# The first modulation rows turned into columns one sum later, through the transposes' PSUM pool

## The chip, the cores and the metric

The kernel runs on one core of a Trainium2 chip. The metric is the device time of one execution in microseconds, the median of several runs. Five engines work side by side, each with a queue of its own that it works off in order: TensorE (PE, and PEld for its weight loads), VectorE (DVE), ScalarE (ACT), GpSimd (POOL) and SyncE (SP), which issues all DMAs here.

## The reference, cut to what matters

One layer of a hybrid backbone is computed for 128 context tokens and 2048 latent tokens of width 1024, all in float32. What the change touches is the modulation at its very start:

```
def modulation(cond, w_mod_l, b_mod_l):
    m = jax.nn.silu(cond) @ w_mod_l + b_mod_l
    return jnp.split(m[:, None, :], N_MOD, axis=-1)
...
    sh1, sc1, ga1, sh2, sc2, ga2 = mod
    h = rmsnorm(x, norm_mix_l) * (1.0 + sc1) + sh1
    o, s_new = mixer(h, s0, n_chunks, w_in_l, conv_l, a_log_l, dt_bias_l, o_norm_l, ws_l, bs_l, w_out_l)
    x = x + ga1 * o
    h = rmsnorm(x, norm_ffn_l) * (1.0 + sc2) + sh2
    x = x + ga2 * (jnp.square(jax.nn.relu(h @ w_ff1_l)) @ w_ff2_l)
```

There are two conditioning vectors, one for the context and one for the latent tokens. Of the six pieces of the modulation, the shift `sh1` and the scale `sc1` are wanted first: no input of the mixer exists before them.

## The kernel before, in words

The 2176 tokens are 17 tiles of 128 rows: tile 0 is the context, tiles 1 to 16 are the latent tokens. The first phase projects blocks of three tiles; the second runs the scans; the third and longest is the MLP, whose matmuls are the lines 220 to 222 with the output `f`.

At the start of the first phase stand four sums of modulation rows. `mod_columns` (L331) makes one of them: 512 columns of `silu(cond) @ w_mod`, over eight slices `k` of the 1024 inputs (L335), with the two conditions as two rows of the PSUM tile `pm`. ScalarE copies the two rows into the tile `mrow` (L337). Four transposes (L340) turn them into columns, 128 of the 512 values at a time, in another `pm` tile. VectorE adds the bias (L343) and, for the scale, adds 1 and multiplies by the norm's weight (L347). What comes out is `b1` (shift) and `a1` (scale), with one column for each slice `k`. The four calls, in the order of the program:

- row 1: shift, half 0 (slices 0 to 3), right behind its loads `m0`
- row 2: scale, half 0, from `m1`, behind the preparation of block 0
- rows 3 and 4: shift and scale, half 1 (slices 4 to 7), from `m2` and `m3`, behind columns 0 to 3 of block 0

The tile `mrow` has one buffer, `pm` two (`pm1`), and `pt` three. `pt` serves all other transposes of the phase, and in block 0 also the sums of the third projection unit. The two `pm` tiles later go to the first sum of `split_mod_steps` (L359, L360) and to the matmuls of `ab_block` (L609, L610).

`column(k)` (L469) prepares slice k of block 0: transposes of the three normalised tiles `x` into a `pt` tile (L482), scale and shift by ScalarE into `full` (L484), then a high and a low part by VectorE, `kH` (L487) and `kL` (L488). Each column is stored to DRAM (L500, L501). The projection units (`feature_tile`) multiply the columns with split weights in three matmuls (L220 to L222), k by k: three units run together over k = 0 to 3, then go on with 4 to 7. `first_half` (L405) scales the halo rows, which GpSimd copies into the edges of the columns (L477, L478). The weights come through `raw_w` (L184) and are split by `split_w` (L191 on ScalarE, L192 on VectorE). `norm_rows` squares (L318), takes the root (L177, L178) and scales (L320) a tile of x, loaded at L392; the tag `x` has three buffers, and the halo tile `xh` (L380, L387) holds one of them first.

The order on each engine isn't the program's. The whole program is handed to a planner (`schedule_with_timeline_sim=True`), which keeps a clock of its own, gives each engine the earliest instruction of the program that is ready by that clock, and hands out the buffers of a tag. Nothing in the first phase fixes an order by hand; in the second, `emit` adds dependences that do.

Of the kernel before, what the change touches and what calls it, by code (L numbers as in the profile page):

```python
# [14 lines left out]
ALU = mybir.AluOpType  # L15
# [3 lines left out]
P = 128  # L19
# [43 lines left out]
def hybrid_step(  # L63
# [7 lines left out]
    V, A, G, T = nc.vector, nc.scalar, nc.gpsimd, nc.tensor  # L71
# [42 lines left out]
    ident = cp.tile([P, P], F32, name="ident")  # L114
# [42 lines left out]
    vec = cp.tile([P, 73], F32, name="vec")  # L157
    a1 = cp.tile([P, 2, KT], F32, name="a1")
    b1 = cp.tile([P, 2, KT], F32, name="b1")
# [11 lines left out]
    def pm1():  # L171
        return pmp.tile([P, 512], F32, tag="pm", name="pm", bufs=2)
# [14 lines left out]
    def split_w(raw, pool=None, tag="w"):  # L187

        h = (pool or wp).tile([P, 512], F32R, tag=tag, name="wH")
        lo = (pool or wp).tile([P, 512], F32R, tag=tag, name="wL")  # L190
        A.copy(h, raw)  # L191
        V.tensor_tensor(out=lo, in0=raw, in1=f32(h), op=ALU.subtract)  # L192
        return h, lo
# [13 lines left out]
    def w512(name, dt=F32):  # L207
        return wp.tile([P, 512], dt, tag="w", name=name)
# [72 lines left out]
    with ExitStack() as ph:  # L281
# [8 lines left out]
        def pt():  # L290
            return ppt.tile([P, 512], F32, tag="pt", name="pt", bufs=3)
# [35 lines left out]
        def mod_load(half, c0):  # L327
            return [raw_w(w_mod[0, k * P : (k + 1) * P, c0 + half * 512 : c0 + half * 512 + 512])
                    for k in range(KT)]

        def mod_columns(raws, half, dst, bias, scaled):  # L331

            pm = pm1()
            for k in range(KT):
                T.matmul(pm[0:2, :], scond[:, k, :], raws[k], start=k == 0, stop=k == KT - 1)  # L335
            row = p1.tile([2, 512], F32, tag="mrow", name="mrow", bufs=1)
            A.copy(row, pm[0:2, :])  # L337
            pc = pm1()
            for i in range(4):
                T.transpose(pc[:, 2 * i : 2 * i + 2], row[:, i * P : (i + 1) * P], ident[0:2, 0:2])  # L340
            ks = slice(half * 4, half * 4 + 4)
            d = dst[:, :, ks]
            V.tensor_tensor(out=d, in0=pc[:, 0:8].rearrange("p (k c) -> p c k", c=2),  # L343
                            in1=bias[:, ks].unsqueeze(1).to_broadcast([P, 2, 4]), op=ALU.add)
            if scaled:
                for cd in range(2):
                    V.scalar_tensor_tensor(out=dst[:, cd, ks], in0=dst[:, cd, ks], scalar=1.0,  # L347
                                           in1=vec[:, 16 + half * 4 : 20 + half * 4], op0=ALU.add, op1=ALU.mult)

        def split_mod_steps(jc):  # L350

# [18 lines left out]
        m0 = mod_load(0, 0)  # L370
        load(out=vec, in_=v_columns)
        convw = vec[:, 32:68].rearrange("p (w a) -> p w a", w=3)
        m1 = mod_load(0, D)
        mod_columns(m0, 0, b1, vec[:, 0:8], False)


        xh = p1.tile([P, D], F32, tag="x", name="xh", bufs=3)[0:10, :]
# [19 lines left out]
        def load_w1(gi, ks):  # L397
            return [w1_raw(gi, k) for k in ks]
# [332 lines left out]
        m2 = mod_load(1, 0)  # L731
        m3 = mod_load(1, D)
        wr = load_w1(1, range(4))
        mod_columns(m1, 0, a1, vec[:, 8:16], True)
        W1[1] += [split_w(r) for r in wr]
        first_half(0)
        abr = p1.tile([P, KT, 16], F32, tag="abr", name="abr", bufs=1)
# [4 lines left out]
        for k in range(4):  # L742
            cols[k]()
            for u in us:
                u["main"][k]()
        mod_columns(m2, 1, b1, vec[:, 0:8], False)
        mod_columns(m3, 1, a1, vec[:, 8:16], True)
        W1[1] += [split_w(r) for r in wk]
        first_half(1)
        for k in range(4, KT):  # L750
# [176 lines left out]
    with ExitStack() as ph:  # L927
# [550 lines left out]
        for i, u in enumerate(units):  # L1478
# [3 lines left out]
            c = i % 2  # L1482
# [107 lines left out]
    def bank():  # L1590
        return psq.tile([P, 512], F32, tag="f", name="f", bufs=8)
# [19 lines left out]
    class Unit:  # L1611
# [121 lines left out]
        def turn(self):  # L1733

            ps = bank()
            for i in range(4):
                T.transpose(ps[:, i * P : (i + 1) * P], self.z0[:, i * P : (i + 1) * P], ident)
            z = w512("zt")
            A.activation(z, ps, AF.Square)
            store(out=z_d[0][0, :, :, 2 * self.jp : 2 * self.jp + 2, :],  # L1740
                  in_=z.rearrange("p (i m t) -> p i m t", i=2, m=2))
# [175 lines left out]
    m0 = {n: [e[0] for e in todo].index(n) for n in range(len(products))}  # L1917
# [43 lines left out]
    half = [p for p, e in enumerate(seq) if e[1] == NP][0]  # L1961
# [9 lines left out]
    for j, t in enumerate(range(8, -1, -1)):  # L1971
        st = h2_steps(t, bank, lambda: junk16, w512, own=own_tile if t == 0 else None)
        p = 16 + 19 * j // 2
# [123 lines left out]
```

## Time and profile before

| | |
|---|---|
| median of 3 runs | 2585.69 us (2585.39 to 2588.91) |
| the profiled execution | 2585.89 us, span 2584.2 us |
| TensorE busy | 2544.6 us, 98% |
| VectorE busy | 1785.2 us, 69% |
| ScalarE busy | 1193.2 us, 46% |
| GpSimd busy | 297.4 us, 12% |
| DMA | 579.77 MB, 224 GB/s on average |

The rows of a timeline give the start and the length in us, the engine, the line, the operation, the tile written and the tiles read, the shape and the count; in brackets stands the idle time ahead of it and what ended that. Consecutive instructions of one kind are merged into one row. Rows of SPq are DMA issues. A group of a view by tiles gives the least, the median and the greatest duration. The tile names are those of the program.

### The profile page before, as it was taken

The page shows a single profiled execution, that of the slowest core. Times are in us where ns is not written, and L with a number is a line of the kernel's source. Part 1 is how long each engine was busy: PE and PEld are TensorE (multiplying, and loading weights), DVE is VectorE, ACT ScalarE, POOL GpSimd, SP SyncE. Part 2 cuts the span into 40 slices and gives each one's busy share as a digit, 9 for nine tenths or more (in the row PEclk, how much of TensorE's full clock was granted, in tenths as well). Part 3 has the DMA queues.
Part 4 walks back from the last instruction along what each step waited for, and adds up shares of the span by engine and source line. Part 5 has one row for each costly group of instructions (what it writes and reads, how often), then busy time and mean ns, then how long its engine had stood idle before and what let it go on. Part 6 is the DMA issues. An engine that isn't in the chain of part 4 may idle for free.

```text
span 2584.2 us, 43725 instructions
## 1 busy us (share of the span) xinstructions
PE 2544.6 (98%) x15296; PEld 2134.3 (83%) x15296; DVE 1785.2 (69%) x3524; ACT 1193.2 (46%) x2758; POOL 297.4 (12%) x512
## 2 busy tenths in 40 slices
PE   8999999999999999999999999999999999999998
PEld 4999999788888878788888888888887888888887
DVE  5877746666667778895587886676665545675874
ACT  4755545554445557763355553333242433243441
POOL 3112112222222222321000000000000000000000
PEclk9999999999999999999999999999999999999999
DMA  8967637755555758996778788454379978786772
GB/s 297 293 217 214 201 115 226 230 166 171 162 173 177 223 180 250 289 310 208 266 221 251 219 288 278 139 152 146 115 224 373 331 267 297 248 257 213 231 254 103
DMA packets 533859, 579.77 MB, mean 224 GB/s; under 512 B 35500, under 2 KB 366684, under 8 KB 530054
## 3 DMA queue, kind: packets, MB, share of 16 engines
q1 hardware_dynamic: 533638, 576.98, 70.1%
q8 instruction: 120, 1.97, 0.3%
q14 instruction: 101, 0.83, 0.1%
HBM read 397.62 MB, written 179.22 MB: 223 GB/s over the span
## 4 chain that ended last, share of the span: by engine, by line
PE 52%; DMA 3%; DVE 1%; issue 1%; ACT 0%; POOL 0%; SPq 0%; DVEq 0%; POOLq 0%; ACTq 0%
PE f L220 16%; PE f L222 16%; PE f L221 16%; DMA r<-in_w_ff_dram 1%; PE pj L220 1%; PE pj L222 1%; DMA zraw<-z_d 1%; PE pj L221 1%; DMA traw<-in_w_ff_dram 0%; PE f L856 0%; PE pd L992 0%; PE pd L1096 0%; PE pd L1060 0%; PE pd L1097 0%; DVE o L1400 0%
## 5 line engine op out<-in xcount | busy, mean ns | idle before, releaser
L220 PE MATMUL f<-hop,zH 128*128 128x512 f32 x960 | 373.6, 390 | 1.9 <-ACT zH L1600 1.8
L222 PE MATMUL f<-hop,zL 128*128 128x512 f32 x960 | 373.6, 389 | 0.0
L221 PE MATMUL f<-hop,zH 128*128 128x512 f32 x960 | 373.2, 389 | 0.0
L220 PE MATMUL f<-hop,wH 128*128 128x512 f32 x896 | 351.6, 393 | 0.6 <-ACT wH L1747 0.6
L221 PE MATMUL f<-hop,wH 128*128 128x512 f32 x896 | 349.0, 390 | 0.0
L222 PE MATMUL f<-hop,wL 128*128 128x512 f32 x896 | 344.0, 390 | 0.0
L1600 ACT CAST zH<-zraw 128x512 fp32r<-128x512 f32 x240 | 147.2, 620 | 298.2 <-DMA zraw<-s_d 87.5
L220 PEld LDWEIGHTS f<-hop,zH 128*128 128x128 f32 x960 | 180.2, 188 | 40.4 <-ACT zH L1600 3.4
L222 PEld LDWEIGHTS f<-hop,zL 128*128 128x128 f32 x960 | 180.2, 188 | 39.1 <-DVE zL L1594 1.7
L221 PEld LDWEIGHTS f<-hop,zH 128*128 128x128 f32 x960 | 180.2, 188 | 37.1
L1594 DVE TENSOR_TENSOR zL<-zraw,zH 128x512 fp32r<-128x512 f32 x240 | 163.1, 689 | 68.6 <-ACT zH L1600 53.7
L222 PEld LDWEIGHTS f<-hop,wL 128*128 128x128 f32 x896 | 168.2, 188 | 35.6
L220 PEld LDWEIGHTS f<-hop,wH 128*128 128x128 f32 x896 | 168.5, 188 | 34.9 <-issue 1.2
L221 PEld LDWEIGHTS f<-hop,wH 128*128 128x128 f32 x896 | 168.5, 188 | 32.3
L222 PE MATMUL pj<-kH,wL 128*128 128x386 f32 (+2 forms) x568 | 190.5, 335 | 0.0
L220 PE MATMUL pj<-kH,wH 128*128 128x386 f32 (+2 forms) x568 | 189.2, 336 | 0.5 <-DVE kH L487 0.3
L221 PE MATMUL pj<-kL,wH 128*128 128x386 f32 (+2 forms) x568 | 189.4, 333 | 0.0
L178 POOL TENSOR_TENSOR r<-rsq,nhalf 128x1 f32<-128x1 f32 (+1 forms) x38 | 22.9, 602 | 1357.1 <-DVE rsq L177 1357.1
L1747 ACT CAST wH<-s 128x512 fp32r<-128x512 f32 x96 | 58.9, 620 | 170.1 <-DVE s L1594 157.0
L537 DVE SCALAR_TENSOR_TENSOR cv<-pj,vec,cv 128x384 f32<-128x384 f32 (+2 forms) x164 | 87.3, 540 | 57.8 <-ACT cv L534 56.5
L220 PEld LDWEIGHTS pj<-kH,wH 128*128 128x128 f32 x568 | 107.1, 189 | 5.1 <-issue 4.7
L221 PEld LDWEIGHTS pj<-kL,wH 128*128 128x128 f32 x568 | 107.4, 189 | 0.5
(408 smaller groups left out, 5718.6 us busy)
## 6 DMA issues: line engine op xcount, KB each, us to landing
zraw<-z_d SPq DMA_DIRECT2D x212, 256.0 KB, 4.5
raw<-in_w_ff_dram SPq DMA_DIRECT2D x128, 256.0 KB, 4.7
hop<-hop_d SPq DMA_DIRECT2D x28, 1024.0 KB, 15.4
z_d<-c SPq DMA_DIRECT2D x96, 256.0 KB, 2.5
zraw<-s_d SPq DMA_DIRECT2D x96, 256.0 KB, 5.3
raw<-in_w_mod_dram SPq DMA_DIRECT2D x80, 256.0 KB, 4.0
r<-in_w_ff_dram SPq DMA_DIRECT2D x80, 256.0 KB, 5.7
s_d<-s SPq DMA_DIRECT2D x64, 256.0 KB, 3.1
```

The lines of the kernel that those rows point to most:

```text
L178: G.tensor_tensor(out=out, in0=t[:np_, :n], in1=nhalf[:np_, :n], op=ALU.pow)
L220: T.matmul(ps, lh, rh, start=first and i == 0, stop=False, skip_group_check=more)
L221: T.matmul(ps, lh, rl, start=False, stop=False, skip_group_check=more)
L222: T.matmul(ps, ll, rh, start=False, stop=last and i == n - 1, skip_group_check=more)
L537: V.scalar_tensor_tensor(out=cv[:, o : o + m], in0=ps[:, s + sh : s + sh + m], scalar=convw[:, w, j : j + 1], in1=cv[:, o : o + m], op0=AL ...
L1594: V.tensor_tensor(out=out, in0=a, in1=b, op=op)
L1600: A.copy(h, src)
L1747: A.copy(h, s2)
```

## The change

`mod_columns` no longer turns its row. It makes the sum and the copy, and hands back a function `turn` that does the rest: the transposes, now in a tile of `pt`, the addition and the multiplies. Each turn is called behind the next row's sum and copy. Row 3's sum moves up, ahead of columns 0 to 3; row 4's stays behind them, and the turns of rows 3 and 4 stand behind it.

```
             row = p1.tile([2, 512], F32, tag="mrow", name="mrow", bufs=1)
             A.copy(row, pm[0:2, :])
-            pc = pm1()
-            for i in range(4):
-                T.transpose(pc[:, 2 * i : 2 * i + 2], row[:, i * P : (i + 1) * P], ident[0:2, 0:2])
...
+            def turn():
+                pc = pt()
+                for i in range(4):
+                    T.transpose(pc[:, 2 * i : 2 * i + 2], row[:, i * P : (i + 1) * P], ident[0:2, 0:2])
+                ks = slice(half * 4, half * 4 + 4)
+                d = dst[:, :, ks]
+                V.tensor_tensor(out=d, in0=pc[:, 0:8].rearrange("p (k c) -> p c k", c=2),
+                                in1=bias[:, ks].unsqueeze(1).to_broadcast([P, 2, 4]), op=ALU.add)
+                if scaled:
+                    for cd in range(2):
+                        V.scalar_tensor_tensor(out=dst[:, cd, ks], in0=dst[:, cd, ks], scalar=1.0,
+                                               in1=vec[:, 16 + half * 4 : 20 + half * 4], op0=ALU.add, op1=ALU.mult)
+
+            return turn
...
-        mod_columns(m0, 0, b1, vec[:, 0:8], False)
+        turn = mod_columns(m0, 0, b1, vec[:, 0:8], False)
...
         wr = load_w1(1, range(4))
-        mod_columns(m1, 0, a1, vec[:, 8:16], True)
+        turn2 = mod_columns(m1, 0, a1, vec[:, 8:16], True)
+        turn()
+        turn = mod_columns(m2, 1, b1, vec[:, 0:8], False)
+        turn2()
         W1[1] += [split_w(r) for r in wr]
         first_half(0)
...
-        mod_columns(m2, 1, b1, vec[:, 0:8], False)
-        mod_columns(m3, 1, a1, vec[:, 8:16], True)
+        turn2 = mod_columns(m3, 1, a1, vec[:, 8:16], True)
+        turn()
+        turn2()
         W1[1] += [split_w(r) for r in wk]
         first_half(1)
```

More of the change, by code (lines that the diff above doesn't have):

```diff
@@ L337, in mod_columns @@
             A.copy(row, pm[0:2, :])
-            pc = pm1()
-            for i in range(4):
[L340 to L348, printed above, removed]
+            def turn():
[11 more added lines that the diff above has]
+            return turn
         def split_mod_steps(jc):
```

## The prediction

> **What bounds the kernel now.** I read the page's line of busy time first, then the busy time by stages (columns: stretch, its length, busy time and instructions of PE, PEld, DVE, ACT, POOL, granted clock, DMA share, GB/s).
>
> ```profile
> PE 2544.6 (98%) x15296; PEld 2134.3 (83%) x15296; DVE 1785.2 (69%) x3524; ACT 1193.2 (46%) x2758; POOL 297.4 (12%) x512
> ```
>
> ```profile
> 41.00:100.00 59.00, 57.55 (x346) 55.56 (x347) 50.90 (x135) 42.94 (x124) 12.38 (x24) 1.00 0.82 260
> 200.00:300.00 100.00, 100.00 (x603) 94.84 (x602) 72.08 (x138) 55.98 (x177) 17.50 (x41) 1.00 0.68 211
> 1240.00:1700.00 460.00, 460.00 (x2139) 383.21 (x2138) 346.08 (x573) 204.49 (x417) 5.21 (x9) 1.00 0.75 239
> ```
>
> TensorE is idle for 2584.2 − 2544.6 = 39.6 us of the span. From 41 us on the first phase keeps it busy for 57.55 of 59 us and then 100 of 100, the last phase 460 of 460. So what TensorE saves before 41 us is handed down nearly whole, and what another engine saves counts only where TensorE waits for it. TensorE's timeline up to there holds all that the change can reach directly.
>
> ```profile
> 4.19 9.37 PE L335 MATMUL pm<-raw,scond 128*2 128x512 f32 x16 [4.19 <-DMA raw<-in_w_mod_dram]
> 14.31 0.38 PE L340 MATMUL pm<-ident,mrow 2*128 2x2 f32 x4 [0.76 <-ACT mrow L337]
> 14.62 7.03 PE L335 MATMUL pm<-raw,scond 128*2 128x512 f32 x16
> 21.57 0.66 PE L387 MATMUL pt<-ident,xh 10*128 10x10 f32 x8
> 22.16 0.33 PE L482 MATMUL pt<-ident,x 128*128 128x128 f32 x1
> 23.35 0.33 PE L482 MATMUL pt<-ident,x 128*128 128x128 f32 x1 [0.85 <-DVE x L320]
> 23.61 0.41 PE L340 MATMUL pm<-ident,mrow 2*128 2x2 f32 x4
> 23.94 7.03 PE L335 MATMUL pm<-raw,scond 128*2 128x512 f32 x16
> 31.69 0.41 PE L340 MATMUL pm<-ident,mrow 2*128 2x2 f32 x4 [0.72 <-ACT mrow L337]
> 32.02 7.03 PE L335 MATMUL pm<-raw,scond 128*2 128x512 f32 x16
> 38.98 0.33 PE L482 MATMUL pt<-ident,x 128*128 128x128 f32 x1
> 39.77 0.40 PE L340 MATMUL pm<-ident,mrow 2*128 2x2 f32 x4 [0.46 <-ACT mrow L337]
> ...
> 41.16 0.59 PE L220 MATMUL pj<-kH,wH 128*128 128x388 f32 x2 [0.33 <-DVE kH L487]
> 41.59 0.34 PE L220 MATMUL pt<-kH,wH 128*128 128x388 f32 x1
> 41.77 0.82 PE L482 MATMUL pt<-ident,x 128*128 128x128 f32 x6
> ```
>
> All four sums (L335) already run ahead of the first projection matmul at 41.16: the planner has pulled the third and the fourth up, although the program has them behind columns 0 to 3. Around them TensorE waits three times for the row's copy by ScalarE (0.76, 0.72, 0.46), once for a normalised tile (0.85), once for the first column (0.33): 3.1 us together, the ceiling of a direct gain.
>
> **The change part by part.** Nothing is added or removed: 64 sum matmuls, 16 transposes, 4 copies, 4 additions, 4 fused multiplies and every DMA stay. The transposes and what follows them move one sum back, the third sum moves up in the program (on the engine it is there already), and the columns take their banks from the three of `pt` instead of the two of `pm`.
>
> First turn. The second sum starts 14.62 − 13.56 = 1.06 us after the first ends (4.19 + 9.37 = 13.56): the copy, then transposes that take 14.62 − 14.31 = 0.31 of the engine. With the transposes behind it, it can start at 13.56 if its rows are there.
>
> ```profile
> 5.71 5.58 SPq L184 DMA_DIRECT2D raw<-in_w_mod_dram  x8
> 16.44 9.99 SPq L184 DMA_DIRECT2D raw<-in_w_mod_dram  x16
> ...
> DMA to landing us min/median/max: 4.7/5.4/5.8
> ```
>
> The last of its eight loads is issued by 11.3 and landed by 11.3 + 5.8 = 17.1, before the sum reaches it, so the sum ends at 13.56 + 7.03 = 20.6 and the turn at 20.9.
>
> Third sum. The halo transposes keep their place (22.16 − 21.57 = 0.59), so it could begin at 21.5. Its first load lands at 16.44 + 5.4 = 21.8 by the median; the others follow 9.99 / 16 = 0.62 apart, and the sum uses one in 7.03 / 8 = 0.88. I take 21.8 to 28.8, against the old end of 23.94 + 7.03 = 30.97. The 0.85 for the normalised tile falls inside it.
>
> Fourth sum. The second row's turn (0.31) and the two early transposes of x (some 0.5) go ahead, then it runs from 29.6 to 36.6, against 39.05 before; its last load lands by 26.43 + 5.8 = 32.2, in time.
>
> What is late next is the third tile of x, whose load stands late in SP's queue, and the way from it to the first projection:
>
> ```profile
> 28.21 0.33 SPq L392 DMA_DIRECT2D x<-in_x_sample_dram  x1
> 34.13 1.06 ACT L318 ACTIVATE junk<-x 128x1024 bf16<-128x1024 f32 x1 [0.64 <-DMA x<-in_x_sample_dram]
> 36.45 0.75 DVE L320 TENSOR_SCALAR x<-x,r 128x1024 f32<-128x1024 f32 x1
> 39.63 0.90 ACT L484 ACTIVATE full<-pt,b,a 128x128 f32<-128x128 f32 x2
> 40.11 0.23 DVE L487 CAST kH<-full 128x128 fp32r<-128x128 f32 x1 [1.51 <-ACT full L484]
> ```
>
> The tile is ready at 36.45 + 0.75 = 37.2, whatever the sums do. Before, its transpose came at 38.98 because the fourth sum held the engine until then; afterwards it can come at 37.2, and the first projection at 37.2 + (41.16 − 38.98) = 39.4: 1.8 earlier. The third and fourth rows' turns (2 × 0.31) then still have to run behind that point, where they ran ahead of it: net 1.8 − 0.6 = **1.2 us**. From below: 0, if the planner keeps the transposes where they wait for the same copies. From above: 3.1, if all the five waits go.
>
> Costs that I set to nothing, and their cover. The columns of half 0 come at about 29 instead of 24.5; behind them stand the halo's scaling on VectorE and its copies on GpSimd, which are wanted by the first column at 39, so 10 us cover them. SP's queue holds nothing that needs these columns before column 0's stores. The row has one buffer, so each copy now waits for the turn of the row before; ScalarE has nothing else to do but the squares and the first weight splits. If that cover went, the second split would be late by one copy, 0.57.
>
> The other half is less safe. Behind 41.59, where the third unit's first matmul takes its bank of `pt`, the transposes of columns 1 and 2 follow at 41.77, though two of the three tiles had been normalised since 23.35: a bank of `pt` is claimed in program order. In the new program the turns of rows 3 and 4 claim theirs behind column 3, and the fourth row's copy waits for the third's turn. So the columns of half 1, added at 40.25 before, come when columns 2 and 3 have left their banks. The rows that price this:
>
> ```profile
> 40.25 0.16 DVE L343 TENSOR_TENSOR a<-pm,vec 128x8 f32<-128x8 f32 x1
> ...
> 42.30 1.72 ACT L484 ACTIVATE full<-pt,b,a 128x128 f32<-128x128 f32 x4 [1.27 <-PE pt L482]
> 43.84 0.49 PE L482 MATMUL pt<-ident,x 128*128 128x128 f32 x3
> 45.73 0.93 ACT L484 ACTIVATE full<-pt,b,a 128x128 f32<-128x128 f32 x2
> 50.98 0.51 PE L220 MATMUL pj<-kH,wH 128*128 128x388 f32 x2
> ```
>
> Columns 1 and 2 are activated from 42.30 to 44.0, so until 42.2 when all is 1.8 earlier; column 3, whose transposes stand at 43.84, takes the bank of column 1, and the third row's turn that of column 2. From there the bare chain is turn 0.31, copy 0.57, turn 0.31, addition 0.16, multiplies 0.24, column 4's activation 0.93 and its two casts 0.7: 3.2 us, ready at 45.4. The matmuls of k = 4 start at 50.98 − 1.8 = 49.2. The slack is 3.8 us, and I take no stall. From below it is 0. From above each of the six steps stands behind one column's whole work on its engine: 2.45 on TensorE and VectorE ((50.98 − 41.16) / 4, the pace of the columns), 1.5 on ScalarE (0.93 and a weight split of 0.6); two steps on each make 12.8 of waits, a stall of 12.8 − 3.8 = 9.0.
>
> **Sum.** The profiled execution took 2585.89; 2585.89 − 1.2 = 2584.7. The median of the runs shown is 0.2 below it, so a median of 2584.5 is forecast.
>
> A rule that speaks against the change, as the trace has it first: in the scan TensorE once stood idle for 5 us, and then ran at half the granted clock for 3.4.
>
> ```profile
> 920.07 0.69 DVE L1437 TENSOR_TENSOR tmp<-pm,row 128x512 f32<-128x512 f32 x1 [5.33 <-DMA row<-mod_d]
> 920.82 1.11 PE L1413 MATMUL pm<-ident,ob 128*128 128x128 f32 x4 [5.04 <-DVE tmp L1437]
> ```
>
> ```profile
> 916.80:920.30 3.50, 0.00 (x0) 0.00 (x0) 0.23 (x1) 0.00 (x0) 0.03 (x1) 1.00 0.60 203
> 920.30:923.70 3.40, 2.88 (x23) 2.63 (x24) 3.40 (x6) 1.73 (x5) 0.00 (x0) 0.50 0.61 234
> ```
>
> The new order would leave TensorE with little to do from 36.6 to 37.2 and from 37.6 to 39.4. [...]
>
> **The rivals.**
>
> No gain (2585.9). The transposes keep waiting: x's third tile is later than I put it, or the turn lands where it was. For it: SP's order is the planner's, and the tile sets the end of the stage. Against it: the copy's waits have no other cause.
>
> [...]
>
> Half 1 is late (2589.8; slower than before). Place: the matmuls of k = 4. Price: the waits in the six steps less the slack of 3.8. It is slower than before from 3.8 + 1.2 = 5.0 us of waits on, slower by 0.2% from 10.2 on; midway between 5.0 and 12.8 the stall is 5.1, so 2584.7 + 5.1. For it: VectorE is busy with 50.90 of 59 us there. Against it: it needs most steps to meet full queues.
>
> The scan's order changes. The planner lays out the whole program again, and a start that is 1 to 2 us earlier can swap two loads. The stall at 920.82 hangs on one late row for L1437 (5.04 idle, and half of the 2.88 busy us at half clock, 1.4: 6.5). Without it 2584.7 − 6.5 = 2578.2; with a second one like it, 2591.2. For it: it is an accident of the queue. Against it: that stage's order hangs on dependences written by hand.
>
> **How the numbers follow.** Chances: forecast 0.47 (2584.5, its own range 2582.6 to 2585.6), no gain 0.18, clock 0.05, half 1 late 0.13, stall gone 0.13, second stall 0.04. A measurement of this kernel can tell about 0.2%, 5.2 us, from no change: faster is below 2580.5, slower above 2590.9. Faster has the stall gone, 0.13. Slower has the second stall, 0.04, and 0.06 of half 1 late. Same: 0.77. The range from 2579 to 2591 leaves out most of the stall gone (0.10), and what lies past 2591 of the other two (0.08).
>
> **What would show it.** Right: the second sum starts at about 13.6 with no wait for a copy; the fourth ends near 36.6; the first projection matmul stands near 39.4; PE's busy time is unchanged at 2544.6 and the span shorter by about 1. Right for half 1: the turns of rows 3 and 4 stand between the columns' transposes behind 41, and PE shows no wait at k = 4. Wrong: a wait of TensorE over 1 us between 37 and 60 us, a clock below 1.00 before 100 us, the third x tile's load at another place in SP's queue, or a shift of the stretches between 470 and 1240 us that the start does not explain.

## The result, and the profile after

The changed kernel is slower. Its median is 2594.53 us (2593.15 to 2599.43, 7 runs), beside 2588.63 us (2585.39 to 2591.81, 7 runs) of the kernel before on the same chip: a ratio of 1.0028, with a 95% interval of 1.0018 to 1.0037, or some 7 us with 5 to 10 as bounds. The forecast was 0.05% faster. The profiled execution took 2594.53 us, its span is 2592.8 us, against 2584.2 us before; these 8.6 us are more than the 7 of the ratio, since the profiled execution of the kernel before was one of its faster ones.

In the new source the lines stand 1 to 7 further down: the transposes of a turn are L341, the addition L344, the halo copies L480 and L481, the transposes of x L485, the scan's L1437 is L1444. `make_masks` (L135, L137), which the prediction did not speak of, makes the masks of the scan on GpSimd; `abW` (L760) holds what the split sum (L362) and `ab_block` multiply with.

The first fence is the page's line of busy time; the second the busy time by stages of the changed kernel, in the columns of the same view before.

```profile
PE 2547.5 (98%) x15296; PEld 2135.6 (82%) x15296; DVE 1787.3 (69%) x3524; ACT 1194.4 (46%) x2758; POOL 293.8 (11%) x512
```

```profile
38.50:41.90 3.40, 3.40 (x13) 3.12 (x13) 1.28 (x6) 1.21 (x4) 0.00 (x0) 0.50 1.04 345
41.00:100.00 59.00, 56.07 (x328) 52.85 (x327) 48.44 (x133) 41.63 (x116) 13.22 (x24) 0.99 0.70 226
100.00:140.00 40.00, 35.92 (x224) 34.22 (x224) 30.27 (x61) 21.98 (x65) 6.00 (x33) 1.00 0.92 304
200.00:300.00 100.00, 100.00 (x602) 94.58 (x601) 71.63 (x137) 53.51 (x169) 17.66 (x42) 1.00 0.61 193
925.90:932.80 6.90, 4.23 (x27) 3.78 (x28) 4.95 (x8) 3.07 (x8) 0.00 (x0) 0.51 0.57 200
1240.00:1700.00 460.00, 459.68 (x2135) 382.47 (x2134) 346.02 (x571) 204.38 (x416) 5.20 (x9) 1.00 0.74 236
```

The same 40 us from 100 on in the kernel before:

```profile
100.00:140.00 40.00, 39.50 (x242) 38.06 (x241) 31.34 (x64) 23.89 (x77) 10.87 (x36) 1.00 0.80 259
```

TensorE has the same work. It does 56.07 us of it between 41 and 100 us, where 57.55 were done before, and 35.92 between 100 and 140 us, where it was 39.50. From 200 on it is as full as ever. Between 38.5 and 41.9 the granted clock is 0.50. So the first phase loses in three places, all before 140 us.

TensorE's timeline shows first that the start went as the change meant it, and then where it waits:

```profile
4.34 15.59 PE L335 MATMUL pm<-raw,scond 128*2 128x512 f32 x32 [4.34 <-DMA raw<-in_w_mod_dram]
...
20.38 0.38 PE L341 MATMUL pt<-ident,mrow 2*128 2x2 f32 x4
21.02 3.60 PE L335 MATMUL pm<-raw,scond 128*2 128x512 f32 x8 [0.26 <-DMA raw<-in_w_mod_dram]
...
25.25 10.46 PE L335 MATMUL pm<-raw,scond 128*2 128x512 f32 x24
...
37.77 0.48 PE L362 MATMUL pm<-wH,abW 128*128 128x512 f32 x1 [1.79 <-DVE abW L760]
38.71 0.98 PE L220 MATMUL pj<-kH,wH 128*128 128x388 f32 x2
...
43.49 0.41 PE L341 MATMUL pt<-ident,mrow 2*128 2x2 f32 x4
...
46.65 0.41 PE L341 MATMUL pt<-ident,mrow 2*128 2x2 f32 x4
...
54.49 0.62 PE L220 MATMUL pj<-kH,wH 128*128 128x388 f32 x2 [1.43 <-POOL kH L480]
...
56.35 0.45 PE L221 MATMUL pj<-kL,wH 128*128 128x388 f32 x1 [0.35 <-POOL kL L481]
```

The first two sums run without a break (32 matmuls from 4.34 to 19.93), the other two nearly so (until 35.71), and the first projection matmul stands at 38.71 instead of 41.16: 2.4 us gained. Then the turns of rows 3 and 4 come at 43.49 and 46.65, where both had run by 40.2 before, and at 53 to 56 us TensorE waits 1.43 and 0.35 us for copies by GpSimd. The view of waits, each group with its total, count and longest time, adds what follows until 140 us:

```profile
PE pj L220 <- DVE cv L540: 3.5, 2, 2.4
PE pj L220 <- POOL kH L480: 1.4, 1, 1.4
PE pj L612 <- DVE cv L540: 0.9, 1, 0.9
...
PE pj L221 <- POOL kL L481: 0.3, 1, 0.3
```

The 3.5 and 0.9 us are waits for a bank of `pj` that VectorE's convolution (L540) has not emptied yet.

How the lag grows is read from the starts of the same matmul in both traces. The changed kernel's 70th projection matmul, at 59 us before, is 2.0 us late; the 208th, at 88, 1.4; the 346th, at 128, 6.2; the 691st, at 209, and the 1728th and last, at 432, 6.1. The first matmul of the MLP, at 1245, is 8.3 late, the last 8.6. So 6.1 us come from the first 130 us, and 2.2 from the scan. Its stall is still there:

```profile
928.57 1.12 PE L1420 MATMUL pm<-ident,ob 128*128 128x128 f32 x4 [5.36 <-DVE tmp L1444]
```

It is 5.36 us long against 5.04, and the half clock behind it lasts for the whole of 925.90:932.80 (0.51 above), twice as long as the 3.4 us of before. e4 and e17 below have some 6.8 us at half clock there too (an estimate from the mean clock: 0.96 in 905:920 and 0.72 in 920:930 in e4, 0.98 and 0.69 in e17) and are not slower, so it is not put down to the change.

GpSimd's timeline, of the changed kernel and then of the kernel before, shows why the copies were late:

```profile
48.08 0.72 POOL L135 TENSOR_SCALAR_AFFINE_SELECT sg<-one 128x128 f16<-128x128 f16 x1 [13.68 <-DVE a L348]
48.75 4.59 POOL L135 TENSOR_SCALAR_AFFINE_SELECT bd<-one 128x128 f16<-128x128 f16 x5
...
54.14 0.65 POOL L480 CAST kH<-halH 128x1 fp32r<-128x1 f32 x4
54.75 0.90 POOL L137 TENSOR_SCALAR_AFFINE_SELECT bd<-bd 128x128 f16<-128x128 f16 x2
55.60 1.37 POOL L481 CAST kL<-halL 128x1 fp32r<-128x1 f32 x4
```

```profile
42.42 1.16 POOL L477 CAST kH<-halH 128x1 fp32r<-128x1 f32 x4 [6.33 <-DVE halH L410]
43.52 0.94 POOL L478 CAST kL<-halL 128x1 fp32r<-128x1 f32 x4
48.23 0.97 POOL L135 TENSOR_SCALAR_AFFINE_SELECT sg<-one 128x128 f16<-128x128 f16 x1 [3.77 <-DVE one L129]
49.16 2.61 POOL L135 TENSOR_SCALAR_AFFINE_SELECT bd<-one 128x128 f16<-128x128 f16 x5
```

Before, GpSimd copied the edges of columns 4 to 7 at 42.4 and made the masks of the scan (L135, L137) from 48.2 on. Now the scale of half 1 is ready only at 48.1, and the masks stand ahead in GpSimd's queue. They also take longer, 4.59 us for five against 2.61. The edges are there at 57.0 instead of 44.5.

```profile
47.09 0.17 DVE L344 TENSOR_TENSOR a<-pt,vec 128x8 f32<-128x8 f32 x1
...
47.92 0.17 DVE L348 SCALAR_TENSOR_TENSOR a<-a,vec 128x4 f32<-128x4 f32 x2
48.13 1.24 DVE L410 TENSOR_SCALAR hal<-hal,a,b 128x10 f32<-128x10 f32 x4
...
49.62 0.41 DVE L413 CAST halH<-hal 128x40 fp32r<-128x40 f32 x1
...
50.41 0.34 DVE L414 TENSOR_TENSOR halL<-hal,halH 128x40 fp32r<-128x40 f32 x1
```

VectorE scaled the halo rows at once (L410) and had split them by 50.8 (L413, L414). Without the masks ahead of them, GpSimd could have begun the copies then.

### The profile page after: what moved, and what is told of

The parts are those of the page before. It is cut to its first block, busy times and chain, and to the rows that moved or that the text cites. A ratio compares the mean times of both kernels' runs of the same rounds, so it can differ in the third digit from the quotient of the medians.

```text
span 2592.8 us, 43725 instructions
## 1 busy us (share of the span) xinstructions
PE 2547.5 (98%) x15296; PEld 2135.6 (82%) x15296; DVE 1787.3 (69%) x3524; ACT 1194.4 (46%) x2758; POOL 293.8 (11%) x512
## 4 chain that ended last, share of the span: by engine, by line
PE 54%; DMA 1%; DVE 1%; issue 1%; ACT 0%; POOL 0%; SPq 0%; DVEq 0%; POOLq 0%; ACTq 0%
PE f L220 16%; PE f L222 16%; PE f L221 16%; PE pj L220 1%; PE pj L222 1%; PE pj L221 1%; DMA zraw<-z_d 1%; PE f L863 0%; PE pd L999 0%; DMA traw<-in_w_ff_dram 0%; PE pd L1103 0%; DMA r<-in_w_ff_dram 0%; PE pd L1067 0%; PE pd L1104 0%; DVE o L1407 0%
## 5 line engine op out<-in xcount | busy, mean ns | idle before, releaser
L221 PEld LDWEIGHTS f<-hop,zH 128*128 128x128 f32 x960 | 180.2, 188 | 37.2
L222 PEld LDWEIGHTS f<-hop,wL 128*128 128x128 f32 x896 | 168.2, 188 | 35.7
L1754 ACT CAST wH<-s 128x512 fp32r<-128x512 f32 x96 | 58.9, 620 | 169.7 <-DVE s L1601 156.5
L540 DVE SCALAR_TENSOR_TENSOR cv<-pj,vec,cv 128x384 f32<-128x384 f32 (+2 forms) x164 | 87.0, 540 | 58.7 <-ACT cv L537 57.5
```

The costliest lines, as they stand in the source:

```text
L221: T.matmul(ps, lh, rl, start=False, stop=False, skip_group_check=more)
L222: T.matmul(ps, ll, rh, start=False, stop=last and i == n - 1, skip_group_check=more)
L540: V.scalar_tensor_tensor(out=cv[:, o : o + m], in0=ps[:, s + sh : s + sh + m], scalar=convw[:, w, j : j + 1], in1=cv[:, o : o + m], op0=AL ...
L1754: A.copy(h, s2)
```

## The experiments

All ratios are to the kernel before, timed between the runs of the changed kernels on the same chip. The theory was that half 1 is the cause: its turns claim banks of `pt` behind columns 2 and 3, so its scale is late, and its edges with it. The rivals: the half clock at 38.5 us, the masks on GpSimd, and the order of TensorE's work that the planner takes.

**Which part of the change.** e3 takes the pool alone and leaves the turns where they were, e4 takes the delayed turns alone and leaves the pool:

```
 e3, in the kernel before      e4, in the changed kernel
-            pc = pm1()        -                pc = pt()
+            pc = pt()         +                pc = pm1()
```

> The kernel before with the columns in the pool of the transposes, each row turned at once as before. Theory A: the turns of rows 3 and 4 then claim their banks behind column 3, half 1 is as late as in the changed kernel, and the waits for the copies (0.76, 0.72, 0.46) stay: 4 to 8 us slower than before. Rival (the pool is innocent, the one sum's delay or the moved third sum costs the time): within 2 us of before.

> The changed kernel with the columns in the old pool pm: one sum later, but no claim of a bank of pt. Theory A: half 1 is turned ahead of the columns, its waits are gone, and the second sum still starts with no wait for the copy: 0 to 2 us faster than before, 5 to 8 faster than the changed kernel. Rival (the delay of one sum itself costs): as slow as the changed kernel.

e3 took 2593.43 us, a ratio of 1.0024 (1.0014 to 1.0034); e4 2587.19 us, 0.9999 (0.9990 to 1.0008). To within 0.1% the delay costs nothing, and the pool alone costs about as much as the whole change. Next, the pool for one half at a time:

```
 e6   +                pc = pt() if half == 0 else pm1()
 e7   +                pc = pt() if half == 1 else pm1()
```

> The changed kernel with rows 1 and 2 turned in pt, rows 3 and 4 in pm. Theory A2 (the claims of pt by rows 3 and 4, behind column 3, are what costs): half 1 is turned ahead of the columns, the first units end near 61 us as before, and the time is that of the kernel before within 2 us, unless the clock falls ahead of the first projection, which adds 1.7 for each 3.4 us at half. Rival (any four claims of pt upset the order): as slow as the changed kernel, +6.

> The mirror: rows 1 and 2 turned in pm, rows 3 and 4 in pt. Theory A2: half 1 is late as in the changed kernel, the halo copies stand behind the masks, the first units end near 68 us: +4 to +7 against before. Rival (rows 1 and 2 cost the time): near before.

e6: 2587.91 us, 1.0001 (0.9992 to 1.0011). e7: 2592.49 us, 1.0017 (1.0007 to 1.0027). To within 0.1%, only half 1 matters. The first copies of its edges on GpSimd, in e6 and in e7:

```profile
40.73 0.54 POOL L480 CAST kH<-halH 128x1 fp32r<-128x1 f32 x4 [6.07 <-DVE halH L413]
```

```profile
52.57 0.65 POOL L480 CAST kH<-halH 128x1 fp32r<-128x1 f32 x4
```

**What is costly about half 1.** e2 takes the masks out of the way, by making them at the very start:

```
         wr = load_w1(1, range(4))
+        make_masks()
         turn2 = mod_columns(m1, 0, a1, vec[:, 8:16], True)
...
-        make_masks()
```

> Only the place of the masks changes: built before the loads of m2 and m3, so GpSimd is free when the halo rows of half 1 are ready. Theory A in its narrow form (the masks in front of the halo copies are the wait): the waits for kH and kL at 53 to 56 us (1.78) go, the rest stays, about 2 us less than the changed kernel. In its wide form (the later waits at 66 and 130 us follow from it too): 4 to 5 us less. Rivals B and C: less than 1 us.

It took 2593.26 us, 1.0022 (1.0012 to 1.0032): nothing was gained. Its timelines of GpSimd and VectorE, and VectorE's busy time over the longest of the copies:

```profile
50.55 7.13 POOL L480 CAST kH<-halH 128x1 fp32r<-128x1 f32 x4 [15.86 <-DVE halH L413]
57.62 0.54 POOL L481 CAST kL<-halL 128x1 fp32r<-128x1 f32 x4
```

```profile
56.78 0.61 DVE L491 TENSOR_TENSOR kL<-full,kH 128x128 fp32r<-128x128 f32 x2
67.98 0.61 DVE L615 COPY absb<-pm 32x128 f32<-32x128 f32 x2 [10.59 <-PE pm L613]
```

```profile
51.65:57.40 5.75, 2.59 (x17) 2.30 (x15) 5.74 (x18) 3.97 (x9) 5.75 (x3) 1.00 0.60 195
```

GpSimd began the copies at 50.55, as soon as the halo rows were split, but four copies of one element per partition took 7.13 us, where e6 needed 0.54. The second of them alone lasted 5.79 us and ended at 57.44. VectorE worked almost without a break until then (5.74 of 5.75 us) and stopped at 57.39. So the masks were only one of two things that stood in the way. The other is read from the two ends alone: the second copy ended 0.05 us behind VectorE's whole run, and not between two of its instructions. This is no rule in these traces: in the kernel before, GpSimd's eight copies between 42.42 and 44.46 took 0.20 to 0.66 us each beside a VectorE that was busy for all of these 2.04 us, and each ended 0.04 us after one of VectorE's instructions. Why the one in e2 lasted through the whole run stays open.

e16 puts the question the other way: the masks stay, and ScalarE makes the edges of columns 4 to 7.

```
                 for col, j in hc:
-                    G.tensor_copy(kH[:, col : col + 1], f32(halH)[:, k, j : j + 1])
-                    G.tensor_copy(kL[:, col : col + 1], f32(halL)[:, k, j : j + 1])
+                    edge = A.copy if bi == 0 and k >= 4 else G.tensor_copy
+                    edge(kH[:, col : col + 1], f32(halH)[:, k, j : j + 1])
+                    edge(kL[:, col : col + 1], f32(halL)[:, k, j : j + 1])
```

> The changed kernel, with the halo copies of columns 4 to 7 on ScalarE in place of GpSimd. Theory 'GpSimd': the late columns cost through these copies, which stand behind the masks and are held up by VectorE's unbroken run; on ScalarE they take their turn at about 51, the waits of 1.43 and 0.35 near 53 and 56 us go, and the time falls to that of the kernel before or at most 1.5 us over it (2586 to 2589). Theory 'late columns': the columns are late whoever copies their edges; then TensorE still waits over 1 us between 48 and 60 us and the time stays 3 us or more over the kernel before.

2590.49 us, 1.0009 (1.0000 to 1.0019). ScalarE's timeline, and TensorE's waits until 140 us:

```profile
48.91 0.47 ACT L481 CAST kH<-halH 128x1 fp32r<-128x1 f32 x4 [0.49 <-DVE halH L413]
...
50.80 0.27 ACT L482 CAST kL<-halL 128x1 fp32r<-128x1 f32 x2
```

```profile
PE pj L220 <- DVE cv L541: 3.0, 3, 1.1
PE pt L553 <- ACT ev L596: 2.2, 1, 2.2
```

The time lies between the two theories. The edges are there at 51.1 instead of 57.0, although the turn of row 4 is still late (the scale is ready at 46.9), and the waits for GpSimd are gone. What is left is 2.4 us over the kernel before. The trace has it in later waits: `pj` banks that VectorE empties late, and 2.2 us for ScalarE near 126 us, which itself waits 3.80 us there for the store of an earlier `ev`. The clock of this trace did not fall at 38 us (1.00 in 38.50:41.90, against 0.50 in the changed kernel's), which is a part of what it gains on that trace: 1.7 us by an estimate, half of the 3.40 busy us at half clock.

**The order of the units.** Ahead of the third unit's last matmul TensorE does 48 projection matmuls into `pj` in the kernel before, which are the first two units' own (24 each), and 68 in the changed kernel, 20 of them of later units. (The expectations speak of 67 or 68 of the fourth unit; 48 of these are the first two's.) e1 turns half 1 early, but still in `pt`:

```
         turn2()
+        turn2 = mod_columns(m3, 1, a1, vec[:, 8:16], True)
+        turn()
+        turn2()
         W1[1] += [split_w(r) for r in wr]
...
-        turn2 = mod_columns(m3, 1, a1, vec[:, 8:16], True)
-        turn()
-        turn2()
         W1[1] += [split_w(r) for r in wk]
```

> Theory A (half 1 comes late): the turns of rows 3 and 4 stand behind column 3 in the claims of pt, so the halo copies of slices 4 to 7 fall behind the masks on GpSimd (waits of 1.43 and 0.35 at 53 to 56 us) and VectorE's work is pushed together later (1.15 at 66, 2.36 at 130). With the fourth sum and both turns ahead of the columns all of these waits are gone: 4.5 to 6 us less than the changed kernel, span about 2587. Rival B (the half clock from 38.5 to 41.9, after the wait ahead of the first projection, is the main loss): that wait stays, so at most 2 us less, span about 2591. Rival C (the loss comes from the scan's order alone): no change in the first phase counts, span 2593.

The edges were there at 42.2, as before the change, and yet it took 2593.44 us, 1.0023 (1.0012 to 1.0034). It has 19 matmuls of later units ahead, a wait of 3.42 us at 65.8 and 10.2 us at half clock before 75 us (0.50 in 39.00:45.80, and 3.4 us from 69.7 on). Either could be the cause. e14 forbids the order: the fourth unit's first matmul may not stand ahead of the third unit's last. e15 does the same in the changed kernel.

```
+                if bi == 0 and j == 6 and k == KT - 1:
+                    third.append(made[-1])
+                if bi == 0 and j == 0 and k == 0:
+                    tc.add_manual_dep(made[0], third[0].name, ...)
```

> The kernel of e1_half1_early, with one order more for TensorE: the fourth unit's first matmul stands behind the third unit's last. Theory 'order': what costs in the early turn of half 1 is that 67 matmuls of the fourth unit run ahead of the third unit's end, so that VectorE gets the finished units late and in a bunch. Then the time falls from 2593.4 to between 2588 and 2590 (the half clock near 39 us may stay and costs up to 3.4). Rival 'clock': the 10 us at half clock before 75 us are the cost; then the time stays within 1.5 us of 2593.4 as long as the half clock stays, and TensorE still waits about 3.4 us near 66 us.

> The changed kernel with the same order for TensorE. Half 1 is still turned late, so its halo copies still stand behind the masks on GpSimd. Theory 'late columns': TensorE now has nothing to put into the wait and idles about 3.5 us between 49 and 60 us; the total stays within 2 us of the changed kernel. Theory 'bunching': the late columns cost only through the bunch of units that they leave, so the waits near 66, 125 and 130 us (1.15, 0.91, 2.36) go and the total is 3 to 5 us less than the changed kernel's.

e14: 2591.07 us, 1.0014 (1.0005 to 1.0024), without any half clock before 900 us (the mean clock of its trace is 0.998, of e1's 0.996), and 1 us over what the theory of the order gave. As order and half clock went together, it doesn't say which of them cost e1 the 2.4 us; some 3.6 us over the kernel before stay without either. e15: 2591.42 us, 1.0019 (1.0009 to 1.0029). Both intervals touch those of the kernels that they came from, so the medians alone don't settle it; the trace of e15 shows what changed, above all in the stretch where the changed kernel did 35.92 us of work:

```profile
41.00:100.00 59.00, 55.36 (x315) 52.76 (x314) 48.03 (x131) 40.64 (x115) 14.09 (x24) 0.94 0.74 235
100.00:140.00 40.00, 39.60 (x245) 38.10 (x244) 31.21 (x63) 24.24 (x75) 7.47 (x34) 1.00 0.91 298
```

The late waits are gone (39.60 us of work), as the theory of the bunch had it; but the edges still stand behind the masks (there at 55.7), and TensorE now idles in front of them (2.02 and 0.89 us), with the half clock behind that (0.94 on the mean of 41 to 100). Each theory was half right. e17 makes both edits, e15's and e16's:

> The changed kernel with both edits, the halo copies of columns 4 to 7 on ScalarE (e16_halo_on_act) and the fourth unit behind the third's end (e15_after_ordered). The trace of e16 has the changed kernel's order after all, 68 matmuls ahead of the third unit's end, and lies 2.4 us over the kernel before; e15 lies 3.9 over it, the changed kernel 5.9. If the copies on GpSimd and the order are two causes that add up, this one lies at 0 to 1 us over the kernel before (2587.5 to 2589). If both edits take away the same loss, it stays at 2 us or more over it, like e16.

2586.27 us against 2585.70, 1.0001 (0.9991 to 1.0010): the loss is gone, with half 1 still turned late and through `pt`. What the late columns cost beyond these two is less than this comparison can show (0.1% either way). No run makes the two edits in the kernel before, so it is not ruled out that they bring a gain of their own which hides a rest of the loss; there the edges are copied by 44.5 and no matmul of a later unit stands ahead already.

```profile
41.00:100.00 59.00, 56.90 (x337) 54.09 (x336) 48.92 (x135) 41.92 (x123) 12.72 (x16) 0.99 0.75 235
100.00:140.00 40.00, 38.73 (x240) 38.01 (x241) 31.10 (x64) 26.29 (x79) 8.34 (x35) 1.00 0.90 297
```

The table sets the runs side by side, each number from the trace of its profiled execution: when the last edge of half 1 is copied, how many projection matmuls of the fourth and later units stand ahead of the third unit's last one, when that one starts, and by how much the last projection matmul of the first phase is later than in the kernel before.

| kernel | edges, us | matmuls ahead | third unit's last, us | lag of the phase, us |
|---|---|---|---|---|
| before | 44.5 | 0 | 58.9 | 0 |
| e10, kernel before with early rows | 43.7 | 0 | 58.1 | +1.9 |
| e4, turns in `pm` | 42.1 | 2 | 57.2 | −0.2 |
| e6, half 0 in `pt` | 42.4 | 2 | 58.8 | −0.1 |
| changed kernel | 57.0 | 20 | 64.9 | +6.1 |
| e7, half 1 in `pt` | 55.4 | 20 | 64.9 | +8.1 |
| e3, `pt` alone | 57.4 | 20 | 65.3 | +5.8 |
| e2, masks early | 58.2 | 22 | 68.3 | +6.3 |
| e15, ordered | 55.7 | 0 | 64.8 | +3.9 |
| e16, edges on ScalarE | 51.1 | 20 | 61.3 | +2.2 |
| e17, both | 52.2 | 0 | 60.0 | +1.3 |
| e1, half 1 early | 42.2 | 19 | 64.6 | +5.4 |
| e14, early, ordered | 42.8 | 0 | 60.6 | +2.9 |

Each lag is that of one execution, and two executions of the same order can differ here: e10, whose edit is in the scan and which is told of below, does the first phase in the same order as the kernel before on TensorE, VectorE, ScalarE and GpSimd, and ends it 1.9 us later. So a difference of 2 us between two rows shows little by itself. The medians bear the larger ones out: over the kernel before on the same chip, the changed kernel lies 5.9 us, e15 3.9, e16 2.4 and e17 0.6.

**The half clock.** e5 gives TensorE two more matmuls into the first bank of the split sum, which its own first matmul overwrites, in the gap near 36 us:

```
+                if k == 0:
+                    for _ in range(2):
+                        T.matmul(u["ps"], ident, raw, start=True, stop=True)
                 T.matmul(u["ps"], abW[:, k, :], h, start=k == 0, stop=False)
```

> The changed kernel with two matmuls more, whose result is overwritten, ahead of the first split sum of the modulation: TensorE has 1.7 us of work in the wait from 36.0 to 37.8 us, and nothing else changes. Theory B1 (part of the loss is the half clock from 38.5 to 41.9 that this wait brings on): the clock stays at 1.00 up to 100 us and the kernel takes 1.5 to 2 us less than the changed one, with the later waits as they were. Theory A1 (all of the loss is the late half 1 and the order that follows from it): no difference, under 1 us.

The half clock at 38.5 went, and the 70th matmul was 0.2 us early instead of 2.0 late; but the time stayed at 2593.22 us, 1.0024 (1.0014 to 1.0034), and the lag of the phase at 5.9. What was gained at 38 was lost again by 135 us, in waits for VectorE's convolution of 4.0 us and another half clock, at 131.8. So e5 does not price the first half clock by itself. e8 adds the same filling to e1:

> Half 1 turned early in pt, as tried before, and the two overwritten matmuls in the wait ahead of the first projection. Theory B1: the early half 1 lost its gain to the clock (6.8 us at half from 39.0, 3.4 more from 69.7: 5.1 us); with the wait filled the first of the two is gone, 3.4 us less than without, near before. Theory A1: no difference to the early half 1 without the filling, +6 against before.

2586.34 us, 0.9996 (0.9987 to 1.0006). Here the planner takes the order of the kernel before, with none of a later unit ahead, so e8 doesn't show that the clock was the cause in e1. Why two short matmuls more bring back that order, and why e14 with the same order is still 2.9 us late, stays open; in e14 the last columns' low parts are written until 58.8, before until 55.0, and VectorE does weight splits ahead of them.

**The stall in the scan.** The prediction had a rival in which a late row for L1437 is the cause of the 5 us stall. e9 loads the gate rows of the context tile earlier, otherwise it is e8; e10 does so in the kernel before, e12 in e4, e18 in e16:

```
+                if cond(t) == 0:
+                    u["ga0"] = [wrow(mod_d[0:1, 2 * D + n * 512 : 2 * D + n * 512 + 512]) for n in range(2)]
...
-                            ga = wrow(mod_d[0:1, 2 * D + n * 512 : 2 * D + n * 512 + 512])
+                            ga = u["ga0"][n]
```

> Half 1 early in pt, the wait ahead of the first projection filled, and in the scan the two gate rows of the context tile loaded in its first step instead of in the step that uses them. If the stall near 915 us (4.7 us idle, then 6.8 us at half clock) hangs on that late load alone, it goes, and the kernel is 6 to 8 us faster than without, 7 to 9 faster than before, about 2579. If another load or the planner's order takes its place: 0 to 2 us.

> The kernel before with the gate rows loaded early and nothing else. The rival of the prediction priced the stall at 6.5 us: 5.0 idle and 1.4 at half clock. If the late load is its cause, 2581 by that price; with 6.8 us at half clock instead of 3.4, as most profiles of these kernels have it, 8 us. If the stall only moves: no change.

> One sum later in the old pool, with the gate rows loaded early. The stall gone, as above, and the start 2 us ahead up to 100 us; if the wait of 2.5 us at 112 us eats that again, as it did without the early rows, the time is that of the kernel before with early rows, within 1 us; if the start's gain is kept, 2 us less.

> The kernel of e16_halo_on_act with the context tile's gate rows loaded early, as in e10_before_rows, where that was worth 4.3 us. The planner takes another order in the first phase here: 68 matmuls of later units ahead of the third unit's end, as in the changed kernel. By 'GpSimd' the copies were the cause and the time is near 2582.5 all the same; if the order costs by itself, the first phase is 3 us or more behind that of e16 and the time is 2585 or more.

e10: 2583.25 us, 0.9981 (0.9972 to 0.9989). e9: 2582.66 us, 0.9977 (0.9969 to 0.9986). e12: 2581.91 us, 0.9976 (0.9965 to 0.9986). e18: 2585.58 us, 0.9986 (0.9976 to 0.9996); as e16 turned out to have the changed kernel's order too, it says nothing on the order. On one chip each, loading the rows early is worth 4.6 us between the medians of the kernel before and e10 (2587.83 to 2583.25) and 4.9 between those of e16 and e18. All three of e9, e10 and e12 are faster than both kernels; e12 (delayed turns in `pm`, early rows) has the lowest median, but is not told apart from e10, so the gain is that of the rows. TensorE around that place in e12:

```profile
905.00:920.00 15.00, 13.72 (x135) 11.33 (x134) 12.05 (x33) 10.12 (x25) 3.44 (x4) 1.00 0.49 161
920.00:930.00 10.00, 10.00 (x95) 8.44 (x92) 9.07 (x15) 5.78 (x18) 4.99 (x5) 1.00 0.89 279
```

It works for 13.72 of 15 us and then without a break, at full clock: the stall is gone.

## Why the prediction was wrong

It forecast 2584.5 us, within 0.2% of no change; the measured ratio is slower by 0.28%.

The start came out nearly as foretold. The second sum follows the first without a wait for a copy, the fourth ends at 35.7 (36.6 foretold), and the first projection stands at 38.71 (39.4). That last agreement is in part luck. The third tile of x was to be ready at 37.2 "whatever the sums do"; it was ready at 35.5, as its load was issued at 26.54 instead of 28.21. What TensorE then waited for was VectorE, which was busy with weight splits: it had `abW` ready only at 37.6 and began to cast the first column (L490) at 38.14. TensorE's busy time, foretold as unchanged, rose by 2.9 us; the longer time at half clock makes some 2.4 of it (an estimate, half of 3.40 + 4.23 − 2.88 busy us in the half-clock stretches of the two traces). That the turns of rows 3 and 4 would claim their banks of `pt` behind the columns', in program order, and so come behind 41 us, was also right: 43.49 and 46.65.

**The step that failed** is the stall at k = 4: "The slack is 3.8 us, and I take no stall." Two things were missing in it. The bare chain was priced at its durations, 3.2 us, and ended at 45.4; in the trace its two turns alone lie 3.2 us apart, column 4's activation starts at 48.15 and the last of its casts ends at 50.5, 7.0 us after the first turn and 1.3 past the 49.2 at which k = 4 was due. That alone was inside the bounds, but the chain was also not the one that decides. The edges of the columns hang on the same scale of half 1, through L410 on VectorE and the copies on GpSimd; the prediction asked what covers them for half 0 only, and never looked what else GpSimd had to do at that time. There were the masks, and, as e2 showed, GpSimd's copy of 5.79 us beside VectorE's run of weight splits and casts. So k = 4 began at 54.49, where TensorE had waited 1.43 us for the edges, and not at 49.2. The rows were there to read: before, the edges of half 1 were copied at 42.42, 5.8 us ahead of the masks, and a delay of the scale by 6.8 us (its addition at 40.25, now at 47.09) turns that around.

**The rival "Half 1 is late"** had the place and nearly the price: 5.1 us of stall against a lag of 6.1 in the first phase. It had 0.13 of the chance, for the reason that "it needs most steps to meet full queues". The chain took 7.0 us in place of 3.2, so some of them did. Its working was wrong in one way that matters for its price: of the 6.1 us only 1.8 are the wait in place. The edges on GpSimd and the order of the units share the rest. In these traces, what each is worth depends on which is taken away first: the edges 3.9 us of the lag (6.1 to 2.2, e16) and then the order 0.9 (2.2 to 1.3, e17), or the order 2.2 (6.1 to 3.9, e15) and then the edges 2.6. As one execution can differ by 1.9 us from the next, only the larger of these steps say much, and the shares stay open. The 1.3 that e17 keeps are not the half clock at 38.7, which it has too (0.52 in 38.50:41.90): its 208th projection matmul is 0.5 us early, and then TensorE waits 2.51 us, until 101.27, for a weight split whose load came late.

**"What TensorE saves before 41 us is handed down nearly whole"** failed as well. e4 is the kernel in which nothing goes wrong: its first projection comes at 39.11, and its 208th projection matmul is still 2.3 us early. Then this row takes it back:

```profile
114.57 0.50 PE L362 MATMUL pm<-wH,abW 128*128 128x512 f32 x1 [2.48 <-ACT wH L191]
```

At that place TensorE waits 2.48 us for a weight split by ScalarE, and the phase ends 0.2 us early. ScalarE is not what paces it: it had itself been idle for 2.32 us, until the load of the modulation's weights had landed.

```profile
113.90 0.62 ACT L191 CAST wH<-raw 128x512 fp32r<-128x512 f32 x1 [2.32 <-DMA raw<-in_w_mod_dram]
```

The kernel before kept TensorE busy for 39.50 of 40 us between 100 and 140 us. That did not prove TensorE to be the bound there: it can have been just late enough for the loads to keep up. So in this trace the gain at the start would have come to nothing even without the loss; the times (0.9990 to 1.0008) can't tell the foretold 0.05% from none.

**The clock** has 0.05 of the chances. No run shows how long TensorE must be idle for it to fall; in the changed kernel it fell to 0.50 in 38.50:41.90, behind 1.79 us of idle time in one piece, which is no longer than the stretch from 37.6 to 39.4 that the forecast itself has ahead of the first projection. By an estimate this cost 1.7 us, half of the 3.40 us at half clock, for all of which TensorE was busy. In e5, where this half clock is gone, the total is as long, with another one at 131.8.

**The scan.** TensorE's order and that of the loads did not change there and the stall stayed, so neither form of that rival came. Its price for the stall was 6.5 us; taking it away brought 4.6 (e10, between the medians).

## What to carry to other kernels

Follow everything that hangs on a value which a change makes late, not only the chain to the next matmul: here a copy of one column on the least busy engine decided, because it fell behind other work there, and in e2 took 5.79 us beside an unbroken run of VectorE. Before counting a saving at the start, look for the next thing that paces the stage, in this case the loads behind ScalarE's weight splits, since a TensorE that is busy nearly all the time can hide a load that is just early enough. Follow a wait one step further than the engine that it names. A pool of buffers that is claimed in program order is a queue; a tile moved into another pool is moved behind all that claims there first.

## What had not been expected of the hardware

The granted clock fell behind much less idle time than the 5.04 us of the stall in the scan. In the changed kernel it fell at 38.51, with 1.79 us in one piece ahead of it, and at 925.98, when 2.77 us of the stall of 5.36 had passed; in e1 it is 0.50 in 39.00:45.80, and it fell again at 69.7, behind a wait of 3.42 us. TensorE's work in the 3.4 us ahead of the fall at 38.51, and of the one at 69.7 in e1:

```profile
35.10:38.50 3.40, 1.57 (x5) 0.51 (x3) 3.40 (x10) 2.08 (x5) 0.00 (x0) 1.00 1.06 345
```

```profile
66.30:69.70 3.40, 0.51 (x3) 0.54 (x4) 2.24 (x6) 2.64 (x6) 0.00 (x0) 1.00 0.97 319
```

So it fell behind 1.57 us of work in one case and 0.51 in the other. e4, with 0.46 us of idle time near 37 us, kept its clock there (1.00 in 38.50:41.90). No single amount of TensorE's work parts the two outcomes in these traces: 1.63 us of work in 3.40 from 130.7 on left the clock of the changed kernel at 1.00 (also in 134.10:137.50), 2.17 in 3.40 from 36.0 on did not in e6 (0.63 in 38.50:41.90). What decides it is not shown.

The other is the copy of e2 that took 5.79 us beside VectorE. That it was VectorE which held it up is inferred from the two ends, 57.44 and 57.39; no run changed VectorE's work alone, and the copies of the kernel before, above, took 0.20 to 0.66 us beside a VectorE as busy.
